# Seven first products instead of six in the mLSTM projection, one group's weights queued behind the operand sums, one weight unit per head split earlier

## The chip, the cores and the metric

The kernel runs on one core of a Trainium2 chip. Its time is the device time of one execution in microseconds; the figure for a kernel is the median of several runs. One more execution was recorded by the hardware profiler; all rows below come from that one. PE is TensorE, DVE VectorE, ACT ScalarE, POOL GpSimd and SP SyncE; SP and POOL issue the DMAs here.

## The reference

A trunk of two layers, an mLSTM layer and an RG-LRU layer, on x of 2048 tokens by 1024 channels in float32. Cut to what the change touches:

```python
u = rmsnorm(x, ln_g[0])
proj = u @ w_in
xm, z, o_pre, i_pre, f_pre = jnp.split(proj, [2048, 4096, 6144, 6148], axis=-1)
xc = silu(causal_dwconv(xm, conv_w, conv_b))
q, k = per_head(xc, w_q) * DK ** -0.5, per_head(xc, w_k)
v = per_head(xm, w_v)                      # 4 heads, DK 256, DV 512
h_tilde = mlstm_chunkwise(q, k, v, log_i, log_f)
hn = group_norm(sigmoid(o_pre) * h_tilde) * norm_w
y = ((hn + skip * xc) * silu(z)) @ w_out
```

Then x + y goes into the RG-LRU layer (projection, convolution, gates, linear scan, output product) and a final RMSNorm.

## The kernel before

Every float32 product is three matmuls of split operands: a value is cast to a high part on ACT and the rest is subtracted on DVE (`split_into`, lines 763 to 770), and `mm3` (364 to 368) adds high by high, high by low and low by high in a PSUM bank of 512 columns.

`phase_a1` (from 389) is the projection u @ w_in, done in two slabs of 1024 tokens by a seven-product scheme of the Strassen kind: the weights come in quarters 11, 12, 21, 22, with four sums and differences of them (s1 to s4), and u in quarters with sums of its own. The operand names of u are u11 and u21, which need no sums, and t1, t2, t3, t4 and u22, which `combos` (215 to 246) makes on DVE and ACT from the second half of the slab: for each of four parts two normalising multiplications, three sums and the splits of t3 and t2, then for all parts the splits of u22, t1 and t4. t4 of part 3 is the last.

A group is one pair of 128-column output blocks: sixteen of them, even numbers xm (followed by the convolution, 12 operations on DVE a group), odd numbers z (only a SiLU), and beside them four q groups for the o gate. Products 11 by u11 and 12 by u21 need none of the sums. So in each slab `early` (255 to 272) does these two products for the first NE = 6 z groups (1, 3, 5, 7, 9, 11) while the sums are made, keeping product 11 of each in a work buffer `p1` (`wk`, ten buffers, line 68). Then `group` (274 to 311) does the five others of each of these ("late"), and then come the whole groups of `middle`: q0, s0, q1, s2, q2, s4, q3, s6, s8, s10, s12, s14, s13, s15. PSUM has eight banks; a group's evictions (line 278 and the copies on ACT) are on DVE and ACT and leave through `wk` buffers to DRAM, z by POOL's queue (611).

The weights of the groups are fetched in the order of the list `order` (403 to 405) by `prefetch` (408 to 414), under high priority, one to two groups ahead. `weights` (108 to 140) loads quarters into raw buffers (eight), makes the sums (127) and splits everything into slots (eight). In the first slab the split sums are also stored, by POOL (100), and loaded again in the second. A whole or late group of the first slab costs DVE four sums and, late, five splits. The program gives priorities; the order on each engine is then fixed at compile time by a scheduler, and the helper `order` of line 772 adds an edge that keeps one instruction of an engine behind another. `combos` is issued in the fourth round of `early` in the first slab; the weights of the late groups 1 and 3 are asked for by the first late group's `stream()` (416).

In the middle some side work is hung on positions: the decay rates, the load and norm of the next slab's tokens (the norm in the group three from the end of the first slab), the gates after q3 of the second slab, and eight units of sums of the output weights in the second slab.

`phase_a2` (780 to 1100) is the recurrence, head by head, in blocks of 256 tokens (two chunks). One turn of the loop at 1072 to 1097 issues, for block b, `recur` of chunk 0, `finish` of the block before, `qk` of the next block, `recur` of chunk 1, then `score` and the value products `v0`, `v1` of the next block. The weights of the next head's value product are asked for in `qk` of that head's first block (925, 926), so in turn 7 of the head before; they go through two raw buffers `wraw` (813). The same two buffers serve the later weights (`later_weights`, 835 to 850): units of the RG-LRU stage that are loaded at one `next(later)` (844) and split in place and stored to DRAM by POOL at the next (846 to 849), in turns 2 to 6 of heads 0 to 2 (turns 0 to 4 of the last head). The first `next` stands at the head of the turn, the second behind `v1`, and the split is ordered behind `self.valued`, the last eviction of a value product issued so far (847). q and k weights of the next head use `wraw` too, in turns 0 and 1 of the head.

Of the kernel before, what the change touches and what calls it, by code (L numbers as in the profile page):

```python
# [38 lines left out]
class Slab:  # L39


    def __init__(self, K, ctx, gain, paired=False, banks=None):
        self.K, self.nc, self.gain, self.paired = K, K.nc, gain, paired
        self.other = {}
        self.wide = 512 if paired else 516
        if paired:
            self.ta = ctx.enter_context(K.tc.tile_pool(name="ta" + gain, bufs=1, reuse_waits="tile"))
        tc = K.tc
        self.tp = ctx.enter_context(tc.tile_pool(name="tp" + gain, bufs=1, reuse_waits="tile"))
        self.rg = ctx.enter_context(tc.tile_pool(name="rg" + gain, bufs=8, reuse_waits="tile"))  # L50
        self.pm = (banks or ctx).enter_context(tc.tile_pool(name="ps" + gain, bufs=8, space=PSUM, reuse_waits="tile"))
        self.rx, self.rxs = self.rg, ExitStack()
        if paired:
            self.rx = self.rxs.enter_context(tc.tile_pool(name="rx" + gain, bufs=8, side="right", reuse_waits="tile"))
        self.places = {}

    def fix(self):

# [34 lines left out]
    def split(self, t, keep=None):  # L93

        w = t.shape[1]
        both = self.slot(w)
        hi, lo = both[:, 0:w], both[:, w:2 * w]
        self.K.split_into(hi, lo, t, "a", "v")
        if keep is not None:
            self.nc.gpsimd.dma_start(keep, both.bitcast(F32))  # L100
        return hi, lo
# [6 lines left out]
    def weights(self, src, keep, again, part=None):  # L108


        if part == "early":
            A = self.raws(src, ("11", "12"))
            return {nm: self.split(A[nm]) for nm in A}
        out = {}
        if again:
            A = self.raws(src, ("22",) if part else ("11", "12", "22"))
            for nm in ("11", "s2", "s3", "12", "s1", "22", "s4"):
                if nm[0] == "s":
                    out[nm] = self.kept(keep[int(nm[1]) - 1])
                elif nm in A:  # L120
                    out[nm] = self.split(A[nm])
            return out
        A = self.raws(src, ("21", "22", "11", "12") if part else ("11", "21", "22", "12"))

        def comb(a, b, op):
            t = self.rx.tile([P, 516], F32, tag="sum", name="sum", bufs=3)[:, 0:512]
            self.nc.vector.tensor_tensor(t, a, b, op=op)
            return t
        if part is None:
            out["11"] = self.split(A["11"])  # L130
        s1 = comb(A["21"], A["22"], ALU.add)
        s2 = comb(s1, A["11"], ALU.subtract)
        out["s2"] = self.split(s2, keep[1])
        out["s3"] = self.split(comb(A["11"], A["21"], ALU.subtract), keep[2])
        if part is None:
            out["12"] = self.split(A["12"])
        out["s1"] = self.split(s1, keep[0])
        out["22"] = self.split(A["22"])
        out["s4"] = self.split(comb(A["12"], s2, ALU.subtract), keep[3])
        return out  # L140
# [24 lines left out]

    def operand(self, nm, j, src, eng):
        hi, lo = (t[:, 0:TB] for t in self.take(nm, j))
        self.K.split_into(hi, lo, src, "a", eng)
        return hi, lo

    def scale(self, xs, rc, row=None, ks=range(KD)):
# [142 lines left out]
class Trunk:  # L314
# [74 lines left out]
    def phase_a1(self, xT, woq, wxz, wout, D):  # L389
        tc, nc = self.tc, self.nc  # L390
        with ExitStack() as ctx:
            S = Slab(self, ctx, "g0")
# [3 lines left out]
            G = tp.tile([P, 2, 64], F32, name="G")  # L396
            hist = tp.tile([P, 16, 3], F32, name="hist")
            nc.vector.memset(hist, 0.0)
            NE = 6
            first = [2 * m + 1 for m in range(NE)]  # L400
            middle = [("q", 0), ("s", 0), ("q", 1), ("s", 2), ("q", 2), ("s", 4), ("q", 3), ("s", 6)]
            middle += [("s", i) for i in (8, 10, 12, 14, 13, 15)]
            order = []
            for s in range(2):
                order += [(k, i, s) for k, i in [("early", i) for i in first[2 * s:]] + [("late", i) for i in first] + middle]
# [2 lines left out]
            def prefetch(n):  # L408
                while order and len(ready) < n + (order[0][0] == "early"):
                    kind, i, s = order.pop(0)  # L410
                    if kind == "q":
                        ready.append(q_weights(woq[i], D["wq"][i], s))
                    else:
                        ready.append(S.weights(wxz[i], D["wx"][i], s, None if kind == "s" else kind))

            def stream(n=2, ahead=True):
                if not ahead:
                    prefetch(n)
                with tc.high_priority():
                    prefetch(n)  # L420
                return ready.pop(0)
# [193 lines left out]
            def out_of(i, s):  # L615
                return (z_out if i % 2 else xm_out)(i // 2, s)

            with tc.high_priority():
                xs, acc = load(0)
                prefetch(1)  # L620
                x1 = ahead(1)
                acc1 = squares(x1, True)
            pb = S.rows(S.invrms(acc))
            U = {}
            for k in range(KD):
                S.scale(xs, None, pb, (k,))
                nm = ("u11", "u21")[k // 4]
# [3 lines left out]
            for s in range(2):  # L631
                t = []
# [4 lines left out]
                def norm():  # L637
                    S.combos(U, x1, *t, held=True)
                p1 = S.early(NE, lambda j: ew[j] if j < 2 * s else stream(1, s), U, lambda j: out_of(first[j], s),
                             ([] if s else [None, None]) + [stat, norm])  # L640
# [139 lines left out]
    def phase_a2(self, wq, wk, wv, rgate, rwout, D):  # L780
# [3 lines left out]
        with ExitStack() as ctx:  # L784
# [50 lines left out]
            def later_weights():  # L835

                parts = [(rgate[i // 2, :, i % 2 * 768:(i % 2 + 1) * 768],
                          [D["gw"][i, :, l * 768:(l + 1) * 768] for l in range(2)]) for i in range(8)]
                parts += [(rwout[k], [D["ow"].rearrange("(h k) p (l n) -> k l p h n", h=2, l=2)[k, l] for l in range(2)])
                          for k in range(12)]  # L840
                for src, keep in parts:
                    n = src.shape[-1]
                    raw, hi = (wp.tile([P, KV * 256], F32, tag="wraw", name="wraw", bufs=2)[:, 0:n] for _ in range(2))
                    self.order(self.loaded, (nc.sync.dma_start(raw, src),))
                    yield
                    a, v = self.split_into(hi.bitcast(F32R), raw.bitcast(F32R), raw, "a", "v")
                    self.order(self.valued, (a, v))
                    for t, k in zip((hi, raw), keep):
                        nc.gpsimd.dma_start(k, t if n == 768 else t.rearrange("p (h n) -> p h n", h=2))
                    yield  # L850
# [189 lines left out]
            def norm(h, b, S):  # L1040
                rs = S["rs"]
                return [nc.scalar.activation(hn, hn, AF.Identity, bias=rs[:, 1, c:c + 1], scale=rs[:, 0, c:c + 1])
                        for c, hn in enumerate(S["hh"])]
# [21 lines left out]
            later = later_weights()  # L1065
            S, steps = project(*blocks[0])
# [4 lines left out]
            late = None  # L1071
            for i, (h, b) in enumerate(blocks):
                if i + 1 < len(blocks):
                    Sn, (loads, qk, score, v0, v1) = project(*blocks[i + 1])
                else:
                    Sn, loads = None, lambda: None
                    qk = score = v0 = v1 = loads
                if late:
                    norm(*late)
                loads()  # L1080
                extra = b < 5 if h == H - 1 else 2 <= b <= 6
                if extra:
                    next(later, None)
                recur(h, b, 0, S)
                if late:
                    finish(*late)
                qk()
                recur(h, b, 1, S)
                score()
                v0()  # L1090
                v1()
                if extra:
                    next(later, None)
                if b < 2 and h < H - 1:
                    head_weights(h + 1, "qk"[b])
                late = (h, b, S)
                S = Sn
# [674 lines left out]
```

## Time and profile before

| | us |
|---|---|
| runs shown (3) | 2933.67, 2934.01, 2935.65 |
| median | 2934.01 |
| profiled execution | 2935.9 |
| its span, first to last instruction | 2934.0 |
| PE busy in it | 2842.4 |
| DVE, ACT, POOL busy | 2128.2, 1518.2, 445.9 |
| mean granted clock of PE | 0.990 |

Roughly by the trace: the first slab of the projection takes 0 to 512 us, the second 512 to 998, the recurrence 998 to 1695 with borders between heads near 1180, 1353 and 1525, the rest 1695 to 2934. In a row of the windows a digit pair such as "26.09 (x97)" is the busy time of an engine and its instructions begun in the window. A row of the waits reads: who waited, for whom, in total, how often, the longest. A line of the timeline has start, duration, engine, source line, operation, output and inputs, and in brackets the idle time ahead of it with what ended it. "SPq" and "POOLq" mark issues of DMAs.

### The profile page before, as it was taken

The numbers are of one execution on the slowest core, as the hardware profiler recorded it, in microseconds if no ns is written. First come the engines' busy times: TensorE is split into PE (matmuls) and PEld (weight loads), VectorE is DVE, ScalarE is ACT, GpSimd is POOL, SyncE is SP. The second block draws the span as 40 slices with busy tenths as digits, with TensorE's granted clock in tenths as the row PEclk, the third lists the DMA queues.
The fourth block names the chain that finished last, engine by engine and source line by source line (L and its number), as shares of the span: only waits on it lengthen the run. The fifth ranks groups of instructions, "written<-read, shape, count | busy, mean of one in ns | idle before, by whom it ended". The sixth has DMA issues, their size and how long they took to land. (4 is left out here: it accounts for less than half of the span.)

```text
span 2934.0 us, 43294 instructions
## 1 busy us (share of the span) xinstructions
PE 2842.4 (97%) x15442; PEld 2438.4 (83%) x15442; DVE 2128.2 (73%) x3594; ACT 1518.2 (52%) x2547; POOL 445.9 (15%) x846
## 2 busy tenths in 40 slices
PE   7999999999999999999999989999999999999998
PEld 5799987889987799898989978887788887778886
DVE  7766789535568588888888866778888657776764
ACT  6354556424445466666666633434434323876761
POOL 1211122101123111111111111001221111000000
PEclk9999999999999999999999999999999999999999
DMA  6766677668898745556666578776776665788865
GB/s 230 264 227 229 245 250 268 193 202 302 264 324 298 257 149 189 175 183 194 194 204 206 175 271 271 245 241 200 257 243 228 220 198 174 289 310 304 285 214 200
DMA packets 295543, 687.36 MB, mean 234 GB/s; under 512 B 29088, under 2 KB 107680, under 8 KB 295328
## 3 DMA queue, kind: packets, MB, share of 16 engines
q1 hardware_dynamic: 228144, 451.13, 47.8%
q0 software_dynamic: 66608, 232.43, 21.1%
q8 instruction: 121, 1.98, 0.3%
q10 hardware_dynamic: 576, 1.05, 0.1%
q14 instruction: 94, 0.77, 0.1%
HBM read 447.32 MB, written 237.17 MB: 233 GB/s over the span
## 5 line engine op out<-in xcount | busy, mean ns | idle before, releaser
L766 ACT CAST s<-raw 128x512 fp32r<-128x512 f32 (+1 forms) x280 | 172.2, 620 | 258.8 <-PE pd L368 68.6
L769 DVE TENSOR_TENSOR s<-raw,s 128x512 fp32r<-128x512 f32 (+1 forms) x280 | 191.5, 688 | 55.3 <-ACT s L766 54.2
L766 ACT CAST u<-t 128x512 fp32r<-128x512 f32 x112 | 68.9, 619 | 167.8 <-PE pc L368 54.8
L366 PE MATMUL acc<-yh,wr 128*128 128x512 f32 x384 | 148.7, 392 | 4.7 <-ACT yh L766 3.2
L367 PE MATMUL acc<-yl,wr 128*128 128x512 f32 x384 | 149.6, 390 | 1.1 <-DVE yl L769 1.1
L368 PE MATMUL acc<-yh,wr 128*128 128x512 f32 x384 | 149.6, 390 | 0.0
L769 DVE TENSOR_TENSOR u<-t,u 128x512 fp32r<-128x512 f32 x112 | 77.0, 690 | 96.1 <-ACT u L766 95.5
L693 DVE SCALAR_TENSOR_TENSOR xc<-xm,vec,xc 128x512 f32<-128x512 f32 x192 | 139.1, 746 | 6.0 <-ACT xc L691 5.3
L766 ACT CAST s<-sum 128x512 fp32r<-128x512 f32 (+1 forms) x120 | 74.0, 618 | 116.5 <-PE pc L368 46.7
L366 PE MATMUL pa<-u,s 128*128 128x512 f32 x304 | 122.2, 403 | 5.6 <-ACT p L265 3.1
L368 PE MATMUL pa<-u,s 128*128 128x512 f32 x304 | 121.7, 401 | 0.0
L367 PE MATMUL pa<-u,s 128*128 128x512 f32 x304 | 121.5, 400 | 0.0
L766 ACT CAST Ch<-C 128x516 fp32r<-128x516 f32 x120 | 74.8, 623 | 86.1 <-DVE da L1017 59.5
L999 DVE SCALAR_TENSOR_TENSOR C<-C,dl,kv 128x516 f32<-128x516 f32 x112 | 83.4, 744 | 46.9 <-PE kv L368 46.9
L693 DVE SCALAR_TENSOR_TENSOR xc<-xr,vec,xc 128x512 f32<-128x512 f32 x144 | 106.0, 747 | 9.2 <-ACT xc L691 7.8
L366 PE MATMUL pj<-vwh,xmh 128*128 128x512 f32 x256 | 104.0, 408 | 3.8 <-ACT vwh L766 3.8
L367 PE MATMUL pj<-vwl,xmh 128*128 128x512 f32 x256 | 102.1, 399 | 2.5 <-DVE vwl L769 2.5
L368 PE MATMUL pj<-vwh,xml 128*128 128x512 f32 x256 | 101.9, 398 | 0.0
L769 DVE TENSOR_TENSOR s<-sum,s 128x512 fp32r<-128x512 f32 (+1 forms) x120 | 82.5, 688 | 25.0 <-ACT s L766 24.2
L366 PEld LDWEIGHTS acc<-yh,wr 128*128 128x128 f32 x384 | 71.8, 188 | 22.3 <-ACT yh L766 4.9
L366 PE MATMUL pd<-u,s 128*128 128x512 f32 x224 | 88.6, 395 | 0.0
L367 PE MATMUL pd<-u,s 128*128 128x512 f32 x224 | 88.5, 395 | 0.0
(499 smaller groups left out, 10013.4 us busy)
## 6 DMA issues: line engine op xcount, KB each, us to landing
wr<-d_ow SPq DMA_DIRECT2D x96, 512.0 KB, 4.5
d_wx<-s POOLq DMA_DIRECT2D x64, 512.0 KB, 4.3
s<-d_wx SPq DMA_DIRECT2D x64, 512.0 KB, 4.3
s<-d_ws SPq DMA_DIRECT2D x64, 512.0 KB, 5.9
raw<-in_wxz_dram SPq DMA_DIRECT2D x124, 256.0 KB, 4.8
d_wr<-s POOLq DMA_DIRECT2D x48, 512.0 KB, 3.6
s<-d_wr SPq DMA_DIRECT2D x48, 512.0 KB, 4.3
raw<-in_rwin_dram SPq DMA_DIRECT2D x94, 256.0 KB, 3.8
```

The lines of the kernel that those rows point to most:

```text
L366: mm(out, sh, mh, start=first, stop=False, skip_group_check=resumed)
L367: mm(out, sh, ml, start=False, stop=False, skip_group_check=resumed)
L368: mm(out, sl, mh, start=False, stop=last, skip_group_check=resumed)
L693: nc.vector.scalar_tensor_tensor(out, x[:, j:j + TB], self.v(wn, m * 4 + j), out, op0=ALU.mult, op1=ALU.add)
L766: a = nc.scalar.copy(hi, src)
L769: b = (nc.gpsimd if lo_eng == "p" else nc.vector).tensor_tensor(lo, src, hi.bitcast(F32), op=ALU.subtract)
L999: nc.vector.scalar_tensor_tensor(C2, C2, self.dl[:, r:r + 1], p2, op0=ALU.mult, op1=ALU.add)
```

## The change

NE becomes 7: z group 13 joins the early and late groups of both slabs and leaves `middle`. The DVE instructions of the weights of the second late group (3) in the first slab are collected (`made`) and ordered behind the last split of the sums (`low["t4", 3]`). In the recurrence the second `next(later)` of turn 6 moves from behind `v1` to ahead of `recur` of chunk 1; in heads 0, 1 and 2, since the last head has none in turn 6.

```diff
-        self.places = {}
+        self.places, self.low, self.made = {}, {}, []
...
-        self.K.split_into(hi, lo, t, "a", "v")
+        self.made += self.K.split_into(hi, lo, t, "a", "v")
...
-            self.nc.vector.tensor_tensor(t, a, b, op=op)
+            self.made.append(self.nc.vector.tensor_tensor(t, a, b, op=op))
...
-        self.K.split_into(hi, lo, src, "a", eng)
+        self.low[nm, j] = self.K.split_into(hi, lo, src, "a", eng)[1]
...
-            NE = 6
+            NE = 7
...
-            middle += [("s", i) for i in (8, 10, 12, 14, 13, 15)]
+            middle += [("s", i) for i in (8, 10, 12, 14, 15)]
...
                     kind, i, s = order.pop(0)
+                    S.made = []
...
+                    if (kind, s) == ("late", 0) and i == first[1]:
+                        self.order((S.low["t4", 3],), S.made)
...
                 qk()
+                if extra and b == 6:
+                    next(later, None)
                 recur(h, b, 1, S)
                 score()
                 v0()
                 v1()
-                if extra:
+                if extra and b != 6:
                     next(later, None)
```

## The prediction

> **What bounds the kernel now.** I read the shares of busy time first, then TensorE's waits stretch by stretch, the windows around each of them, and the timeline where a wait names a late weight.
>
> ```profile
> PE 2842.4 (97%) x15442; PEld 2438.4 (83%) x15442; DVE 2128.2 (73%) x3594; ACT 1518.2 (52%) x2547; POOL 445.9 (15%) x846
> 92.00:150.00 58.00, 57.89 (x250) 46.43 (x249) 41.17 (x64) 22.95 (x37) 15.58 (x29) 1.00 0.74 260
> ```
>
> TensorE (PE) is busy 97% of the span, and the change leaves its work as it is. So the time can move only by the 2934.0 - 2842.4 = 91.6 us in which PE is idle, and by the stretches in which its clock is low. The second row (columns: window, length, then busy time and count of PE, PEld, DVE, ACT, POOL, then granted clock, DMA share, GB/s) gives the unit of account at full clock: 58.00/250 = 0.232 us a matmul, so a product of 12 is 2.78 us, an early group of two products 5.57 us, a whole group of seven 19.5 us.
>
> The change touches two places where PE loses time: the start of the first slab, and the three borders between heads in the recurrence.
>
> **The start of the first slab: one more early group, and weights behind the sums.**
>
> ```profile
> PE pc L366 <- ACT t3h L766: 2.4, 1, 2.4
> PE pd L366 <- DVE u L278: 0.9, 1, 0.9
> ...
> 59.03 0.40 PE L368 MATMUL pa<-u21h,s 128*128 128x512 f32 x1
> ...
> 59.40:90.20 30.80, 26.09 (x97) 18.79 (x95) 29.82 (x50) 15.12 (x26) 4.73 (x9) 0.89 0.65 231
> ...
> 88.21 0.68 DVE L769 TENSOR_TENSOR t4l<-x,t4h 128x512 fp32r<-128x512 f32 x1
> 89.41 0.68 DVE L278 TENSOR_TENSOR u<-pb,p 128x512 f32<-128x512 f32 x1
> ...
> L769 DVE TENSOR_TENSOR s<-sum,s 128x512 fp32r<-128x512 f32 x9 | 6.1, 684 | 0.1
> L127 DVE TENSOR_TENSOR sum<-raw 128x512 f32<-128x512 f32 x6 | 4.1, 684 | 0.7 <-DMA raw<-in_wxz_dram 0.7
> L769 DVE TENSOR_TENSOR s<-raw,s 128x512 fp32r<-128x512 f32 x3 | 2.1, 687 | 0.8 <-ACT s L766 0.8
> L127 DVE TENSOR_TENSOR sum<-sum,raw 128x512 f32<-128x512 f32 x3 | 2.0, 682 | 0.0
> L127 DVE TENSOR_TENSOR sum<-raw,sum 128x512 f32<-128x512 f32 x2 | 1.4, 681 | 0.0
> ```
>
> From the end of the early products (59.4) to the first eviction (89.41, so PE goes on at 90.2) PE ran 97 matmuls, 97 x 0.232 = 22.5 us of work in 30.8 us: 8.3 us lost. 97 is about 8 x 12: all eight PSUM banks were full (the wait on u L278), and DVE evicted none until the sums were done (the last split, t4l, at 88.21). The single waits inside matter less than that end: DVE is full (29.82 of 30.80), 0.60 us an operation. The five grouped rows (DVE from 47.9 to 88.9) are weight work among the sums: 23 operations; nine (four sums, five splits) are the second late group's.
>
> The change: (1) the early products end 5.57 us later, at 65.0; (2) DVE gets two more splits before the sums, +1.2 us; (3) nine operations go behind t4l, -9 x 0.60 = -5.4 us. The eviction comes at 90.2 + 1.2 - 5.4 = 86.0, plus three sums of the second group, which are now queued at t4l and may go first: 87.8. The new wait holds up on DVE only weight operations, and through them that group's four stores on POOL's queue and its products. So PE has less to do meanwhile: the first and the third late group only, 6 banks, 72 x 0.232 = 16.7 us, in 87.8 - 65.0 = 22.8 us: 6.1 us lost, a gain of 2.2. If some other weights fill the two banks (5.6 us) the gain is 7.8. If the third group is not ready either, PE has 8.4 us of work, while DVE, without that group's operations, ends some 4 us sooner: 22.8 - 4 - 8.4 = 10.4 lost, a cost of 2. I take -3, near the two-group case, which the buffers allow (eight raw buffers, four to a late group); ends -8 and +2.
>
> **The light group taken out of the middles.** The z group 13 stood between the last xm group and the last z group of both slabs.
>
> ```profile
> 391.00:512.00 121.00, 120.00 (x524) 96.69 (x523) 112.22 (x205) 69.16 (x116) 35.86 (x65) 1.00 0.77 266
> 920.00:968.00 48.00, 48.00 (x208) 38.75 (x207) 45.20 (x87) 27.05 (x41) 16.54 (x31) 1.00 0.97 326
> 968.00:998.00 30.00, 29.29 (x127) 23.36 (x125) 8.28 (x12) 10.18 (x17) 4.19 (x8) 1.00 0.57 176
> ```
>
> First slab's last six groups: PE 121 us, DVE 112.2. Without group 13 (PE 19.5; DVE five evictions and eleven weight operations, 16 x 0.60 = 9.7) it is 101.5 us of PE and 102.5 of DVE: DVE ends 1.0 us late, 8.4 if its present idle time (8.8 us, by length 7.4) stays. Against that, and 1.2 us for the two splits, the seventh early group of the second slab puts 5.57 us in front of the first product that needs the sums: 1.0 + 1.2 - 5.6 is below nothing, 8.4 + 1.2 - 5.6 = +4.0. PE has no wait there on a late sum to win back, so no gain. I take +1. End of the second slab: DVE is full to 968 (its backlog from the last xm group) and then nearly idle for 30 us; the backlog, some 10 us, now falls into the last group's 19.5 us. I take +0.5, ends 0 and +3 for loads of the next stage that wait for its late stores.
>
> **The borders between heads: one unit split sooner.** Here a unit of later weights is loaded into `wraw`, split and stored; its two buffers are the ones that the next head's value weights (v) are loaded into.
>
> ```profile
> 1321.98 0.35 SPq L844 DMA_DIRECT2D wraw<-in_rwout_dram  x1
> 1337.63 1.05 ACT L766 CAST wraw<-wraw 128x1024 fp32r<-128x1024 f32 x1
> 1338.97 0.81 POOL L849 DMA_DIRECT2D d_ow<-wraw  x1 [3.57 <-ACT wraw L766]
> 1341.02 0.73 POOL L849 DMA_DIRECT2D d_ow<-wraw  x1 [1.24 <-DVE wraw L769]
> 1343.12 4.59 SPq L814 DMA_DIRECT2D wraw<-in_wv_dram  x2
> 1348.50 1.05 ACT L766 CAST vwh<-wraw 128x1024 fp32r<-128x1024 f32 x1 [3.09 <-DMA wraw<-in_wv_dram]
> ...
> 1336.53 0.75 DVE L999 SCALAR_TENSOR_TENSOR C<-C,dl,kv 128x516 f32<-128x516 f32 x1 [1.73 <-PE kv L368]
> ...
> DMA to landing us min/median/max: 4.0/4.9/6.3
> ```
>
> This is the second border. The unit was asked for at 1321.98 and landed by about 1326.9 (median 4.9), yet was cast at 1337.63, since the split stands behind the block's last products. Its stores went out at 1338.97 and 1341.02, the v loads only at 1343.12 and, after SP had waited inside the second, at about 1347.4; ACT then waited 3.09 us for the first, with kT behind it in its queue. With the split ahead of the block's second chunk the cast comes at about 1327, some 10 us sooner; the stores land by about 1335, before SP's turn. What that removes:
>
> ```profile
> PE pt L1052 <- ACT hh L1042: 2.5, 2, 2.2
> PE s L937 <- ACT kT L923: 0.6, 1, 0.6
> PE pj L367 <- DVE vwl L769: 0.5, 1, 0.5
> ...
> PE s L937 <- ACT kT L923: 1.7, 1, 1.7
> PE pj L366 <- ACT vwh L766: 1.6, 1, 1.6
> PE pj L367 <- DVE vwl L769: 0.5, 1, 0.5
> ...
> PE pj L366 <- ACT vwh L766: 1.9, 1, 1.9
> PE s L937 <- ACT kT L923: 0.8, 1, 0.8
> PE pj L367 <- DVE vwl L769: 0.5, 1, 0.5
> ...
> 1181.67 0.33 SPq L863 DMA_DIRECT2D qb<-d_q  x1
> 1186.50 0.40 POOL L894 TENSOR_SCALAR_AFFINE_SELECT qb<-qb 128x256 f32<-128x256 f32 x1 [11.11 <-DMA qb<-d_q]
> ```
>
> The three triples are PE's waits at the first, second and third border: 3.6, 3.8 and 3.2 us. The pt wait of the first hangs on the same chain: qb is queued on SP behind loads that wait for `wraw`, POOL stands 11.11 us on it, and the norm behind that is late. Sum 10.6 us. Then the clock:
>
> ```profile
> 1350.00:1354.00 4.00, 1.79 (x13) 1.55 (x14) 3.48 (x7) 2.79 (x5) 0.00 (x0) 1.00 1.03 306
> 1354.00:1360.00 6.00, 5.47 (x17) 4.04 (x17) 3.99 (x10) 2.02 (x7) 1.31 (x4) 0.72 0.85 272
> 1526.00:1534.00 8.00, 7.48 (x21) 5.59 (x20) 4.51 (x11) 3.37 (x7) 1.30 (x4) 0.57 0.57 181
> ```
>
> After PE was busy 1.79 of 4.00 us the clock was 0.72 for 6 us, and 0.57 for 8 us after the third border: (1 - 0.72) x 6 + (1 - 0.57) x 8 = 1.7 + 3.4 = 5.1 us. With the waits gone, this goes too: 15.7 us in all. [...]
>
> What it costs: the split's cast (1.05 us) and subtraction (1.2 us) stand ahead of the second chunk's state update on ACT and DVE; they leave the end of the block, and DVE still waits for PE at the next chunk (1.73 us at 1336.53). Bound: nothing, or 1.2 us at each of three borders if PE waits for the update behind it. I take 0.5 each, 1.5. ACT may stand up to 1 us on a unit not landed; nothing behind it is needed before the next chunk. What is late next is vwl on DVE and hh, about 0.5 us a border: 1.5 us. Net -15.7 + 3.0 = -12.7; ends -15.7 and -5 (the clock term and half the waits stay).
>
> **Sum.** -3 + 1 + 0.5 - 12.7 = -14.2 us. The profiled execution took 2935.9 us with a span of 2934.0; the median of the runs shown is 2934.01, so I take the sum from that: 2920 us.
>
> **The rivals.** A: the split does not move in effect. It may be issued earlier and still be queued behind the same products, or the v loads keep their place on SP's queue behind another load. Then only the slabs move: -3 + 1.5 = 2932.5, no change that can be measured (this kernel's bound is about 0.2%, 5.9 us). For it: SP's queue is in order. Against: the load landed 10 us before the cast, and SP stood inside L814 for the store. 0.15.
>
> B, the slower one: the shared work buffers. Ten serve all intermediate results; seven first products now hold seven.
>
> ```profile
> d_sz<-z POOLq DMA_DIRECT2D x12, 256.0 KB, 4.7
> 78.13 1.13 POOL L100 DMA_DIRECT2D d_wx<-s  x2 [15.01 <-DVE s L769]
> ```
>
> Of the three left, a late group wants one for u2 and one for each z until its store has landed, 4.7 us after its issue, and POOL's queue can stand (15.01 us here) on a weight split with z stores behind it. It decides once a z buffer is away for longer than two products (5.6 us) plus what the banks hold. Price: the 15 us stand in each slab, 30 us, against -12.7 in the recurrence and no gain at the start: +17, 2951. Against: with six held, no wait of PE names such a buffer, and each late group gives one back. 0.07.
>
> C: the recurrence gains, the slabs cost: +2 at the start, +4 and +3 for the missing light groups, -12.7: 2930; in the milder half still below 2928. 0.18. The forecast itself: 0.60, with 2910 (-15.7 and -8) as its far end.
>
> **How the numbers follow.** 2910 is the forecast's far end; 2932 takes in C and half of A, and leaves out B and the rest of A. Faster: 0.60 + half of C + a little of A with a better start, 0.72. Same: most of A and half of C, 0.20. Slower: B and the rim of C, 0.08.
>
> **What would show it.** Right: near 1327 a cast of `wraw` ahead of the block's second chunk; v loads 3 us or more sooner against the block; vwh, vwl and kT gone from PE's waits at the borders; clock 1.00 there; early products ending near 65 and the loss up to the first eviction under 7 us. Wrong: the v load still following the store by its landing; a wait of PE on p, u or z buffers in the late groups; PE waiting for u11, t2 or sums near 500 to 560; a larger hole than now around 998.

## The result, and the profile after

| | before | after |
|---|---|---|
| median of the runs, us | 2934.54 (6 runs) | 2955.59 (6 runs) |
| profiled execution / its span | 2935.9 / 2934.0 | 2957.01 / 2955.2 |
| up to the first o product, one group (19.5 us) more after | 151.9 | 170.7 |
| from there to the first o product of the second slab | 479.4 | 490.5 |
| from there to the first product of the recurrence, one group less after | 367.0 | 347.7 |
| the recurrence, to its last state product | 685.7 | 697.2 |
| the rest | 1250.1 | 1249.2 |

After over before is 1.0064 (95%: 1.0054 to 1.0074): the kernel became slower, where 2920 us was forecast. The stretches are read off the starts of PE's products in the two traces; "o product" is the first product of a q group. They place the loss: of 21.2 us of span, 11.5 lie in the recurrence and 11.1 between the first o products; nearly all of these 11.1 are at the border between the slabs, as the waits below show. The other stretches make up for 1.4.

The page's first line of shares, after: PE was busy 6.7 us longer with the same number of instructions, which fits the lower granted clock (0.987 on the mean, 0.990 before), and its gaps grew by 14.5 us.

```profile
PE 2849.1 (96%) x15442; PEld 2447.0 (83%) x15442; DVE 2130.2 (72%) x3594; ACT 1516.4 (51%) x2547; POOL 444.1 (15%) x846
```

**The start of the first slab.** The waits of PE from 62 to 100 us:

```profile
PE pb L366 <- ACT s L769: 3.8, 1, 3.8
PE pd L367 <- DVE t1l L772: 1.7, 1, 1.7
```

The timeline of the same stretch:

```profile
65.18 0.39 PE L366 MATMUL pb<-t2h,s 128*128 128x512 f32 x1
74.54 2.49 DVE L772 TENSOR_TENSOR t4l<-x,t4h 128x512 fp32r<-128x512 f32 x4
77.55 0.68 DVE L278 TENSOR_TENSOR u<-pb,p 128x512 f32<-128x512 f32 x1
79.53 0.49 PE L366 MATMUL pb<-t2h,s 128*128 128x512 f32 x1 [3.84 <-ACT s L769]
```

The early products end at 65.2, the sums at 77.0 (t4l), the first eviction follows at 77.55 instead of 89.41. PE's last wait is no longer for an eviction, but for the weights that were put behind the sums (s on ACT, 3.84 us).

**The border between the slabs.** PE's waits from 490 to 535 us (before: 0.7 us in all):

```profile
PE pa L366 <- ACT p L288: 4.7, 1, 4.7
PE pd L366 <- DVE z L278: 2.0, 1, 2.0
PE pa L366 <- ACT p L265: 1.2, 1, 1.2
```

The timeline around the first of them:

```profile
505.27 0.62 ACT L769 CAST s<-raw 128x512 fp32r<-128x512 f32 x1 [2.01 <-DMA raw<-in_wxz_dram]
507.80 0.74 DVE L696 SCALAR_TENSOR_TENSOR xc<-xm,vec,xc 128x512 f32<-128x512 f32 x1
508.57 0.63 ACT L601 ACTIVATE xc<-xc 128x512 f32<-128x512 f32 x1 [0.59 <-DVE xc L696]
509.82 0.56 ACT L288 COPY p<-pa 128x512 f32<-128x512 f32 x1
510.43 0.79 PE L366 MATMUL pa<-u21h,s 128*128 128x512 f32 x1 [4.71 <-ACT p L288]
```

The window around all three:

```profile
500.00:532.00 32.00, 24.06 (x93) 18.57 (x92) 23.08 (x41) 18.16 (x32) 5.40 (x10) 0.89 0.57 203
```

The copy of product 11 of the last group (15) comes only after the SiLU of group 14's convolution, which DVE delivers late. Group 13, which gave DVE 9.8 us of slack at this place (19.5 us of PE with 9.7 us of DVE work), is gone. ACT also stands 2.01 us on a weight of the next slab that has not landed. PE works only 24 of 32 us, and the clock is 0.89: 0.57 from 510 to 514 us, 0.80 from 518 to 522 and 0.78 from 522 to 526. The waits (7.9 us against 0.7) and the low clock ((0.43 + 0.20 + 0.22) x 4 = 3.4 us lost) make 10.6 of the 11.1 us.

**The first border between heads.** In the rows that follow, vwh and vwl are the high and low part of the next head's value weights, qh and kT come from its q and k, and pt is the transpose of a finished block (hh) after its norm. The norm needs the roots (frs), which POOL computes; POOL also puts a mask on each block's decay rows (qb) when they have landed. The timeline:

```profile
1173.82 1.32 SPq L817 DMA_DIRECT2D wraw<-in_wv_dram  x2
1175.24 0.56 SPq L866 DMA_DIRECT2D qb<-d_q  x1
1181.13 0.40 POOL L897 TENSOR_SCALAR_AFFINE_SELECT qb<-qb 128x256 f32<-128x256 f32 x1 [12.81 <-DMA qb<-d_q]
1182.89 0.19 POOL L1041 TENSOR_TENSOR frs<-frs 128x2 f32<-128x2 f32 x1
1183.12 0.81 ACT L1045 ACTIVATE hh<-hh,frs 128x512 f32<-128x512 f32 x1 [8.56 <-POOL frs L1041]
...
1204.53 0.41 POOL L897 TENSOR_SCALAR_AFFINE_SELECT qb<-qb 128x256 f32<-128x256 f32 x1 [1.65 <-DMA qb<-d_q]
```

The same mask and roots in the kernel before:

```profile
1163.50 0.20 POOL L1038 TENSOR_TENSOR frs<-frs 128x2 f32<-128x2 f32 x1
1163.75 0.42 POOL L894 TENSOR_SCALAR_AFFINE_SELECT qb<-qb 128x256 f32<-128x256 f32 x1
```

PE's longest wait from 1165 to 1215 us:

```profile
PE pt L1055 <- ACT hh L1045: 7.0, 4, 3.7
```

The window, with the clock at 0.80:

```profile
1179.00:1213.00 34.00, 27.01 (x161) 25.06 (x160) 22.11 (x40) 19.55 (x36) 4.24 (x11) 0.80 0.46 150
```

The waits for vwh and vwl are gone, as forecast. But the wait for pt grew from 2.5 to 7.0 us: POOL stands 12.81 us on the mask of a later block's qb, and behind it in POOL's queue come the roots (frs) that the norm of the current block needs. Before, the roots stood ahead of that mask. It is not the mask on which POOL stood 11.11 us before: that one belongs to the next block (1204.53 here), it stands ahead of the next roots in both kernels, and its wait has fallen to 1.65 us. Away from the borders each mask comes right behind the roots of the block five before its own. In the kernel before, that one mask broke this order; after, four masks do, at all three borders. From the last root of a head's sixth block to that of the next head's second block, the three borders take 86.2, 87.9 and 88.5 us before and 93.8, 88.6 and 90.0 us after, so that most of the loss is at the first.

**The second border.** The timeline:

```profile
1341.93 0.34 SPq L847 DMA_DIRECT2D wraw<-in_rwout_dram  x1
1347.72 1.04 ACT L769 CAST wraw<-wraw 128x1024 fp32r<-128x1024 f32 x1 [3.55 <-DMA wraw<-in_rwout_dram]
1348.67 0.61 ACT L769 CAST qh<-qd 128x512 fp32r<-128x512 f32 x1
1349.19 0.58 ACT L926 COPY kT<-pj 128x512 f32<-128x512 f32 x1
1349.82 1.22 PE L940 MATMUL s<-qT,kT 128*128 128x128 f32 x4 [2.14 <-ACT kT L926]
```

The moved cast stands in ACT's queue ahead of qh and kT and waits there 3.55 us for its unit, asked for only 5.8 us earlier; PE's scores wait 2.14 us for kT. The third border looks alike.

### The profile page after: what moved, and what is told of

Read it like the earlier page. It is cut to its first block, busy times and chain, and to the rows that moved or that the text cites. A ratio compares the mean times of both kernels' runs of the same rounds, so it can differ in the third digit from the quotient of the medians.

```text
span 2955.2 us, 43312 instructions
## 1 busy us (share of the span) xinstructions
PE 2849.1 (96%) x15442; PEld 2447.0 (83%) x15442; DVE 2130.2 (72%) x3594; ACT 1516.4 (51%) x2547; POOL 444.1 (15%) x846
## 5 line engine op out<-in xcount | busy, mean ns | idle before, releaser
L366 PE MATMUL pd<-u,s 128*128 128x512 f32 x224 | 88.5, 395 | 0.0
```

The source lines that it names most:

```text
L366: mm(out, sh, mh, start=first, stop=False, skip_group_check=resumed)
```

## The experiments

Theory: two separate losses. In the recurrence (Q) the earlier split was bought with a worse order in ACT's and POOL's queues; in the projection (D) the first slab's end depended on the slack that z group 13 gave DVE. The rivals are named with each run. All times of a run stand beside runs of the kernel before on the same chip; the last four columns are the first four stretches of the first table, in us. With seven first products 19.5 us belong to the first of these four instead of the third. The stretches come from one profiled execution of each kernel, which can lie some 4 us off the median (the candidate's took 2937.10 us, that of the order alone 2936.10, that of the masks 2937.72), and in the five variants that keep the projection of before the first three differ by up to 1.4 us from one another.

| kernel | median us | over before (95%) | to 1st o | o to o | to recurrence | recurrence |
|---|---|---|---|---|---|---|
| earlier split alone | 2945.58 | 1.0036 (1.0022–1.0049) | 153.8 | 479.4 | 368.5 | 696.6 |
| seven, ordered | 2944.28 | 1.0032 (1.0021–1.0044) | 169.8 | 489.8 | 347.9 | 685.7 |
| order alone | 2939.77 | 1.0016 (1.0007–1.0025) | 155.3 | 479.4 | 368.4 | 683.9 |
| seven, not ordered | 2945.61 | 1.0039 (1.0026–1.0052) | 170.7 | 491.7 | 348.3 | 684.0 |
| q group between | 2943.03 | 1.0030 (1.0019–1.0041) | 169.3 | 488.0 | 349.9 | 684.9 |
| copy first | 2945.21 | 1.0040 (1.0027–1.0052) | 171.3 | 487.9 | 347.0 | 685.1 |
| taps left out | 2939.18 | 1.0012 (1.0002–1.0021) | 169.9 | 485.0 | 349.4 | 684.8 |
| q groups spread | 2951.60 | 1.0048 (1.0035–1.0062) | 171.3 | 494.1 | 348.6 | 686.7 |
| cast behind kT | 2933.64 | 0.9998 (0.9989–1.0007) | 152.9 | 479.9 | 368.6 | 684.9 |
| masks behind roots | 2933.63 | 0.9993 (0.9982–1.0003) | 152.9 | 479.7 | 369.0 | 684.8 |
| both | 2928.82 | 0.9975 (0.9966–0.9984) | 152.6 | 479.4 | 369.6 | 677.9 |
| split between v0 and v1 | 2929.34 | 0.9982 (0.9973–0.9991) | 152.4 | 479.3 | 368.7 | 678.4 |
| candidate with seven | 2932.84 | 0.9990 (0.9982–0.9999) | 170.4 | 484.2 | 351.1 | 680.3 |

### The parts one by one

The earlier split alone: only the hunk at the end of the change's diff.

> Only the earlier split of the unit in turn 7; the projection is that of before. Theory Q (the earlier split stands in the wrong place of three queues at each border, whatever the projection does): the recurrence is 11 us longer than before (border 1 the most, 7 to 8 us), first pj at 998, time about 2945, ratio 1.0035 to 1.005. Rival N (the recurrence loses only because the scheduler, with the longer projection in front, lays the borders out otherwise): the recurrence gains the 12 us I forecast, time about 2922. Rival 0: the recurrence loses less than 3 us by itself, time 2934 to 2937.

Seven first products with the ordered weights: all the other hunks.

> Seven first products and the ordered weights, the recurrence's code as before. Theory D (with z group 13 gone from the middle, DVE falls behind at the end of the first slab, and the norm for the next slab is late): first pj near 1009 instead of 998, the recurrence 685 to 686 us as before, time about 2944 to 2945, ratio 1.0035. Rival 0: the projection loses nothing by itself and the time is within 3 us of 2934.

The order alone: as that, but with NE = 6 and the old `middle`.

> Six first products as before, but the second late group's weights ordered behind the last split of the sums. Theory D (the order costs little; the loss is the missing light group's): within 2 us of 2934 with the end of the first slab as before. Rival E (the order itself costs, since PE then has one late group instead of two to run while the sums are made, 5.6 us of early work less than with seven): start of the first slab 4 to 8 us longer, time 2938 to 2942.

Seven without the order: only

```diff
-            NE = 6
+            NE = 7
-            middle += [("s", i) for i in (8, 10, 12, 14, 13, 15)]
+            middle += [("s", i) for i in (8, 10, 12, 14, 15)]
```

> Seven first products, no ordered weights. Theory D: the same loss of about 10 us at the border between the slabs, and a start of the first slab that is as good as with the order or 1 to 5 us better (two late groups in reach): 2940 to 2945. Rival E (the order is what costs): 2926 to 2934, faster than before by the early products that fill the start.

The first two came out at Q's and D's numbers: 10.4 and 9.1 us above the 2935.16 of before, together 19.5 of the change's 21.0. The parts add up; rival N (the borders suffer only from the longer projection) falls. The order alone costs 4.6 us by the medians, which is E's figure and not D's, though the start in its trace is only 1.5 us longer than with the earlier split alone. But with seven products the order makes no difference that the runs can tell (2944.28 against 2945.61, where E had 2926 to 2934), and the loss at the slabs' border is there without it: 491.7. The order is not what costs here.

### The recurrence: which queue

The cast ordered behind kT:

```diff
                     self.order(self.valued, (a, v))
+                    self.order((self.kT,), (a,))
```

> The earlier split alone, with the projection of before, and the split's cast ordered behind the copy kT on ACT; the value loads still stand ahead of the next block's qb and o on SP; on POOL the mask of qb goes behind the roots (frs) at the first border as a by-product. Theory Q (it is the place of the cast ahead of qh and kT, and of the mask ahead of the roots, that costs): the waits of s on kT and of kv go at borders 2 and 3, the wait of pt on the norm shrinks at border 1; the recurrence goes from 696.6 to between 680 and 688 us, time 2928 to 2936. Rival L (the value loads that stand on SP ahead of qb and o cost it): the recurrence stays above 692, time 2941 or more.

The masks ordered behind the roots, the cast left where the change puts it:

```diff
-                    nc.gpsimd.affine_select(qb, qb, ...
+                    t = nc.gpsimd.affine_select(qb, qb, ...
+                    if len(self.roots) > 3:
+                        self.order(self.roots[-4], (t,))
...
+                    self.roots.append(self.rooted)
```

> The earlier split alone, projection of before; on POOL each mask of a qb is ordered behind the roots (frs) that it stands behind in the kernel before, so POOL's queue is the old one; the cast still stands ahead of qh and kT on ACT, and the value loads ahead of qb and o on SP. Theory QP (POOL's order is what costs the first border, ACT's order the other two): the waits of pt on the norm near 1180 and 1200 go, 5 to 7 us of the 11; the waits of s on kT and of kv at borders 2 and 3 stay; recurrence 689 to 692 us, time 2938 to 2941. Rival QA (the cast's place on ACT explains all, and the mask is a by-product): recurrence stays above 694, time 2943 or more.

Both orders:

> The earlier split alone, projection of before, with the cast ordered behind kT on ACT and every mask ordered behind the roots on POOL; what still differs from the split between the two value products is that the value loads stand ahead of qb and o on SP and that the split is done sooner. Theory QP: the waits of pt at borders 2 and 3 (1.0 and 2.4 us with the cast alone put right) go too; recurrence 677 to 681 us, time 2927 to 2930, as with the split between the value products. Rival L (SP's order costs as well): recurrence 683 to 686, time 2933 to 2935.

The split between the two value products, no order added:

```diff
                 v0()
+                if extra and b == 6:
+                    next(later, None)
                 v1()
-                if extra:
+                if extra and b != 6:
```

> The split put between the two value products instead of ahead of the second chunk, projection of before: it is then tied to the first value product of its own block, the cast goes behind kT, and the value loads keep their place behind the next block's qb and o. Theory Q: with all three queues in the old order and the cast some 5 us sooner than before, the waits on vwh at borders 2 and 3 (1.6 and 1.9 us) and part of the low clock go; recurrence 676 to 683 us against 685.6 before, time 2925 to 2932. Rival T (an earlier split brings nothing in any place, since what is late behind it takes over): recurrence within 2 us of 685.6, time 2933 to 2936.

POOL's order alone takes the recurrence from 696.6 to 684.8, more than I expected of it (689 to 692); the cast's order alone, with the mask of the first border put right as its by-product, to 684.9; both together to 677.9. The cast's place is thus worth 6.9 us once POOL is in order (4.8 by the medians). The waits of PE with the masks behind the roots, at the first border, then the third:

```profile
PE n L366 <- DVE hh L1024: 1.2, 1, 1.2
PE kv L366 <- DVE C L1001: 0.4, 1, 0.4
PE pt L1055 <- ACT hh L1045: 0.3, 1, 0.3
...
PE s L939 <- ACT kT L925: 2.6, 1, 2.6
PE kv L366 <- DVE C L1001: 1.1, 2, 1.0
```

pt is down from 7.0 to 0.3 us, and s still waits for kT: each queue has its own wait. With both orders neither is left (PE's waits at the second border):

```profile
PE kv L366 <- DVE C L1002: 1.6, 3, 1.3
PE kv L367 <- DVE vl L970: 0.8, 1, 0.8
PE pt L1056 <- ACT hh L1046: 0.3, 1, 0.3
```

And the window there, with its clock at 1.00 where before and after had 0.97 and 0.94:

```profile
1330.00:1390.00 60.00, 57.13 (x406) 52.84 (x405) 50.01 (x90) 40.93 (x78) 8.98 (x19) 1.00 0.58 193
```

Rival L falls: here the value loads still stand ahead of qb and o on SP, in the split between v0 and v1 they stand behind both, and the recurrences are 677.9 and 678.4. SP's order costs nothing that shows. Rival T falls too. With the split between v0 and v1 the scheduler left the value loads behind qb and o, and put the cast behind kT; on POOL no mask breaks the usual order any more. The cast finds its unit landed (it has no wait), 10 us ahead of the cast of vwh:

```profile
1337.69 1.05 ACT L766 CAST wraw<-wraw 128x1024 fp32r<-128x1024 f32 x1
1338.77 1.23 DVE L769 TENSOR_TENSOR wraw<-wraw 128x1024 fp32r<-128x1024 f32 x1 [0.23 <-ACT wraw L766]
1340.22 1.54 POOL L849 DMA_DIRECT2D d_ow<-wraw  x2
1343.56 0.55 SPq L814 DMA_DIRECT2D wraw<-in_wv_dram  x1
...
1347.36 1.05 ACT L766 CAST vwh<-wraw 128x1024 fp32r<-128x1024 f32 x1 [1.68 <-DMA wraw<-in_wv_dram]
```

Both kernels, this one and the one with both orders, beat the kernel before and the change. One rival stays open. In both, POOL's queue is better than that of before, where one mask at the first border stood 11.11 us ahead of the roots; so the order that the masks were given is not just the old one, as their expectation has it. With both orders the three borders take 83.9, 85.3 and 84.6 us, and the 2.3 us gained at the first against before may come from that mask alone, without the earlier split. No run orders the masks in the kernel before, and the same recurrence code took 89.1 us there in the kernel with seven ordered products.

### The projection: why the first slab's end is late

A q group between the last xm and the last z group (first slab only):

```diff
+            mids = [middle[:6] + middle[7:12] + [("q", 3), ("s", 15)], middle]
-                for j, (kind, i) in enumerate(middle):
+                for j, (kind, i) in enumerate(mids[s]):
```

> Seven first products and the ordered weights as in the kernel with these alone (9 us slower than before), but in the first slab the q group 3 goes from ahead of xm group 6 to between the last xm group 14 and the last z group 15; the second slab is unchanged. Theory D (the 10.5 us lost between the first o products of the two slabs come from the convolutions of group 14 standing directly ahead of the last group's evictions, with no group of few operations between them): that stretch goes from 489.8 back to 480 or 481 us, the time from 2944 to about 2934 or 2935. Rival H (the loss comes from what seven early products ahead of the second slab need, the held buffers or the sums for it being late): the stretch stays at 488 or more, time 2942 to 2945.

A priority for the copy:

```diff
+            with ExitStack() as e:
+                if "u21" in mid:
+                    e.enter_context(self.K.tc.high_priority())
-            self.nc.scalar.copy(p1, a)
+                self.nc.scalar.copy(p1, a)
```

> Seven first products and the ordered weights as in the kernel with these alone, and only the copy of product 11 of the first slab's last group gets a high priority. Theory A (the copy stands in ACT's queue behind two SiLUs that wait for DVE's convolutions, and PE waits 3.6 us for it): the wait of 3.6 us on that copy and the low clock behind it go, 4 to 6 us of the 10.5; the waits on DVE of 2.0 and 1.2 us stay: time 2938 to 2940. Rival B (DVE as a whole is late; PE waits for the next eviction instead): the wait moves to DVE's sums, time 2942 to 2945.

Both missed. With the q group between, the border itself is nearly clean (0.8 us), but the loss moves to the q group, which waits on DVE for the eviction of an xm group and for the scaling of the next slab's tokens (x), and on ACT for a copy (PE's waits from 440 to 530 us):

```profile
PE ob L366 <- DVE xm L278: 3.4, 1, 3.4
PE oa L366 <- ACT p L565: 1.7, 1, 1.7
PE ob L366 <- DVE x L178: 1.4, 1, 1.4
PE pa L366 <- ACT p L265: 0.8, 1, 0.8
```

The priority changed nothing: the copy still comes behind the SiLUs, with a wait of 3.5 us. So its place in ACT's queue is not chosen for want of priority; that it needs one of the ten work buffers, which group 14 holds until its convolutions are done, fits, but was not tried by itself.

Less work for DVE, three of four taps of group 14's convolution left out:

```diff
-                        self.conv(xc, x, "mcw", "mcb", m)
+                        self.conv(xc, x, "mcw", "mcb", m, 1 if (m2, s) == (7, 0) else 4)
```

> Seven first products and the ordered weights, as in the kernel with these alone; left out are three of the four taps of the convolution of xm group 14 in the first slab, twelve DVE instructions of 0.75 us or 9 us of DVE work, about what the missing z group 13 gave DVE as slack. Theory D (DVE's backlog from the five xm groups in a row, which z group 13 used to absorb, holds the work buffer and the evictions of the last group): the stretch between the first o products of the two slabs goes from 489.8 to 479 to 482 us, the wait on the copy p goes, time about 2935. Rival H (the loss belongs to the last group's own loads and to the sums for the next slab): the stretch stays above 487.

The wait on the copy goes, as D said, but the stretch falls only to 485.0, about half of the way. What is late next is another thing (PE's and ACT's waits near the border):

```profile
PE pd L366 <- DVE z L278: 3.6, 1, 3.6
PE pa L366 <- ACT p L265: 0.9, 1, 0.9
...
ACT s L769 <- DMA raw<-in_wxz_dram: 4.3, 2, 3.0
```

ACT stands on weights of the next slab that have not landed, DVE behind it, and the eviction of z behind both. The DMA engines are full there (share 1.04 from 500 to 510 us). So D holds for half; that the other half is the loads of the next slab, which now have one group less to arrive in, is read from this trace and not shown by a run of its own.

The q groups spread, and last the candidate: spread, the call that loads the next slab's tokens and sums their squares two groups later, and the split between v0 and v1.

```diff
+            spaced = [(k[0], int(k[1:])) for k in "q0 s0 s2 q1 s4 s6 q2 s8 s10 q3 s12 s14 s15".split()]
+            mids = [spaced, middle]
```

> Seven first products and the ordered weights; in the first slab the q groups are spread among the xm groups (q0 s0 s2 q1 s4 s6 q2 s8 s10 q3 s12 s14 s15), so that two xm groups stand in a row ahead of the last z group instead of five. The second slab is unchanged. Theory D (a backlog that grows with the number of xm groups in a row): the stretch between the first o products falls from 489.8 to 480 to 484 us, adjusted for the place of the q groups by the waits of PE from 400 to 530 us, and the time to 2933 to 2937. Rival E (the whole slab is too full for DVE without z group 13 in its middle, wherever the q groups stand): PE's waits move to other groups and the time stays at 2941 to 2945.

```diff
-                    if s == 0 and j == 5:
+                    if s == 0 and j == 7:
                         xs, acc = load(2)
```

> A candidate for the best: the split between the two value products, seven first products and the ordered weights, the q groups spread in the first slab, and the load of the next slab's tokens two groups later (with xm group 8 instead of ahead of q group 2, where DVE stood on a weight behind that load and PE waited 6.6 us). Theory D: no wait of PE above 2 us between 200 and 500 us; the start gives 3.6 us, the border between the slabs costs about 3, the second slab gives 1: time 2926 to 2930, the same as with the split between the value products alone. Rival E (without z group 13 in its middle the first slab is too full for DVE and DMA wherever things stand): another wait of 3 us or more comes up in the middle or at the border, time 2933 to 2940.

The first made a new hole and missed its expectation. PE's longest wait from 330 to 352 us:

```profile
PE ob L366 <- DVE xm L278: 6.6, 1, 6.6
```

That window:

```profile
330.00:352.00 22.00, 15.40 (x89) 13.88 (x88) 17.83 (x36) 9.62 (x18) 5.35 (x10) 0.82 0.57 204
```

DVE stood 2.81 us, up to 344.91, on a weight that SP issued only near 339 us, and the eviction stood behind it in DVE's queue. The tokens' load is not ahead of that weight, as the expectation of the candidate has it: in both kernels SP issues the load between 67 and 78 us. What the later call moves is the squares of the tokens on ACT and their sums on DVE, from 322 to 331 us, just ahead of the hole, to 369 to 382 us. With them moved the hole is gone, and PE's waits at the border (490 to 530 us) are down to

```profile
PE pd L366 <- DVE z L278: 2.0, 1, 2.0
PE pa L366 <- ACT p L288: 1.3, 1, 1.3
PE pa L366 <- ACT p L265: 1.2, 1, 1.2
```

with a clock of 1.00: the stretch is 484.2, 5.6 us better than 489.8 and still 4.8 worse than with six. So the order of the groups, with the squares moved, gives back half of this stretch. But the next stretch, up to the recurrence, is 351.1 us against 347.9, with a wait of 3.3 us for an eviction (1.6 us with seven ordered products); of the 5.6 us 2.4 are left. Whether the candidate or only this execution has that wait, one trace cannot tell. At 2932.84 the candidate is nearer to rival E's time than to D's; it beats the kernel before by a little, but not the kernels with the split alone put right (2928.82 on the same chip). I found no order in which seven first products pay; what the last 4.8 us are made of stays open.

## Why the prediction was wrong

**The start (-3): right in sign.** Over six executions with the old start (before, and the five with the projection of before; 151.9 to 153.8) and seven with the new (169.3 to 171.3, less 19.5), the means are 152.8 and 150.9: -1.9 us. That is no more than the spread of either set, so the size is uncertain. The working differs from the forecast in both halves: PE had only one late group to run (the "third group not ready either" of the text), but the first eviction came at 77.55, not at 86 to 88.

**"I take +1" for the missing light group: the first step that failed.** The text put DVE's backlog at up to 8.4 us, but then set the 5.57 us of the seventh early group against it, as though the first to suffer were the first product that needs the next slab's sums. The wait came earlier, in the last group itself: its copy of product 11 and its evictions stand behind group 14's convolutions. So nothing is subtracted: in the kernel with seven ordered products alone the stretch is 10.4 us longer (489.8 against 479.4), in place of 1, in waits for the last group's copy and evictions and in a low clock (0.84 from 510 to 520 us) that the sum had no term for. DVE's backlog is shown for about half of it, by the taps left out. That q groups or DVE work elsewhere did not give it all back fits with the light group having also given the next slab's loads their time; no run shows that by itself.

**End of the second slab (+0.5): right.** Executions of either kind take 368.5 and 368.3 us there (one group counted alike).

**The borders (-12.7): the second step that failed.** "ACT may stand up to 1 us on a unit not landed; nothing behind it is needed before the next chunk": it stood 3.55 us, and behind it were qh and kT, which PE needed next. And the first border's pt wait, of which it says that it "hangs on the same chain", was counted as gone: POOL did wait less for the mask meant there (11.11 to 1.65 us), but the wait for pt grew to 7.0 us, since POOL's queue was laid out anew and the mask before that one came ahead of the roots and held them up for 12.81 us. So -12.7 became +11.5. I followed the moved step itself through the queues, but not what the scheduler would put elsewhere once the split was no longer tied to its own block's last value product. That the late unit cost time was right: with both queues in order the recurrence gains 7.7 us, up to the rival named above. That is the clock's 5.1 us at the borders in full (from 1330 to 1390 us it is 1.00 against 0.97, over the execution 0.992 against 0.990), and waits that fall from 12.5 to 8.2 us (the rows of the three borders, small kv and n waits included); I had left only 3.0 us of waits and costs standing. Of these 9.4 us, 1.7 are given back elsewhere in the recurrence; its first block takes some 0.8 us longer in that execution.

**The rivals.** A (no effect) and B (buffers in the late groups, 0.07) did not happen; C had the slabs' cost about right (9 us; measured -1.9 + 10.4 - 0.2 = 8.3), but by luck, since its parts were +2, +4 and +3, and it had the recurrence on the wrong side. Slower came by a case that none of them named: an earlier instruction of little worth, in the way of others that PE waits for. The sign that I had named, PE waiting near 500 to 560, did come, but for a copy and evictions, not for u11, t2 or sums as I had written.

## What to carry to other kernels

An instruction that is issued sooner stands on its engine ahead of others, and they wait with it: here qh and kT stood 3.55 us behind the moved cast on ACT, and the roots 12.81 us behind a mask on POOL. List what stands behind it, and ask whether it can wait there for a DMA; then look at the other queues, since a scheduler that orders the program anew may move more than the step that was edited. A light piece of work between two heavy ones is slack for the engine that is not the bound (z group 13: 9.7 us of DVE work in 19.5 us of PE), and it may also be time for the transfers of the next stage; before it is spent elsewhere, the gain there has to be weighed against the backlog that it no longer takes up. A loss of this kind can be mended by an order edge on each queue concerned, or by a place that leads the scheduler to a good order, and it pays to try that before the idea is given up.

## What the runs showed of the clock

Idle stretches of PE went with different clocks behind them. In the kernel before, PE was busy 1.79 of 4.00 us from 1350 us, where waits of 1.7 us for kT and 1.6 us for vwh end, and the clock was 0.72 over the next 6 us, a loss of (1 - 0.72) x 6 = 1.7 us. A wait of 2.2 us for hh that ends at 1189.37 left PE busy for less, 1.46 of 4.00 us, and the clock was 1.00 there and behind it:

```profile
1186.50:1190.50 4.00, 1.46 (x11) 1.06 (x11) 0.70 (x1) 2.00 (x4) 1.72 (x5) 1.00 0.06 21
1190.50:1197.00 6.50, 6.50 (x58) 6.50 (x57) 6.44 (x11) 5.74 (x12) 0.00 (x0) 1.00 0.25 81
```

In the kernel after, the wait of 3.7 us at the same border ends at 1183.99, and the clock was 0.76 around it and 0.56 behind it:

```profile
1180.50:1184.50 4.00, 0.48 (x1) 0.18 (x1) 0.06 (x1) 1.38 (x3) 1.71 (x5) 0.76 0.16 62
1184.50:1190.00 5.50, 4.83 (x25) 4.83 (x26) 4.54 (x7) 5.50 (x10) 0.00 (x0) 0.56 0.27 90
```

With the split between v0 and v1, PE was busy 1.97 of 4.00 us from 1180 us, and the clock was 1.00 there and over the next 8 us. So neither the length of a wait nor PE's busy time in 4 us told in these traces what the clock would be behind it; what sets it was not shown. That the low clock at the borders would go with the waits was the author's estimate; with both orders the window from 1330 to 1390 us has 1.00.
